# Low parts of FFN weights in a hybrid diffusion step: a subtraction on VectorE replaced by an accumulating DMA

## The chip, the cores and the metric

The kernel runs on one core of a Trainium2 chip. The metric is the device time of one execution in microseconds (us). The profile gives, beside that, the span from the first to the last instruction, and the TensorE clock that was granted in each stretch as a share of full speed.

## What is computed

The reference is one step of a two-layer backbone over 640 tokens (512 latent, 128 context) of width 1024, all in float32. Layer 0 mixes with an S5 scan and neighbourhood attention, layer 1 with a bidirectional SSD scan; after each mixer stands a SwiGLU FFN. The change lies in the FFN alone:

```python
def _swiglu(h, w_gate, w_up, w_down):
    return (jax.nn.silu(h @ w_gate) * (h @ w_up)) @ w_down

# for each layer:
ffn = (ffn_w_gate[layer], ffn_w_up[layer], ffn_w_down[layer])
xs = xs + gtf_s * _swiglu(_modulate(_rmsnorm(xs, norm_ffn_g[layer]), shf_s, scf_s), *ffn)
```

`w_gate` and `w_up` are 1024 x 2816 (22 column blocks of 128), `w_down` is 2816 x 1024.

## The kernel before

TensorE multiplies float32 in a rounded form (F32R). To keep precision, each operand is split in two: a high part `hi` (the value rounded to F32R) and a low part `lo = x - hi`. A product is then three matmuls for each 128-row step k: hi·xh, hi·xl and lo·xh. `split` (L187 to L189) makes the two parts: ScalarE (ACT) copies and rounds to `hi`, then VectorE (DVE) subtracts to get `lo`. Weights arrive from HBM by `raw_w` (L286) into one of two `wraw` buffers, on the queue of SyncE (SP). `split_w` (L291) takes a `whi` and a `wlo` tile, three buffers each, that the whole kernel shares.

Column blocks 0 to 3 of each FFN are computed straightforwardly. Blocks 4 to 21 go through `block_pair` (L438): gate and up of one block are computed together, with the halves of the contraction and of the tokens as the blocks of a 2 x 2 by 2 x 2 product, in seven block products of 12 matmuls (128x128 weights, 320 columns) instead of eight. There are 18 pairs in each layer, 36 in all. A pair loads `rg` (gate) and `ru` (up), 512 KB each; with `a`, `b` the halves of `rg` and `c`, `d` those of `ru` DVE forms the sums `s1 = c+d`, `s2 = s1-a`, `s3 = a-c`, `s4 = b-s2` in single buffers (tiles `fws` and `fsc`). The weights of the seven products are `ab` (`rg` split, 128x1024), `s12` (128x1024), `s34` (two halves, 128x512 each) and `d` (128x512, in its own tile `fwd`). A `whi`/`wlo` pair is free for the next pair's use once both products that read it are done. The token side lies ready in seven forms (`fm`). In the order of the code the products are: ab with forms 0 and 1, s12 with 5 and 4, s34 with 6 and 2, d with 3; ACT and DVE combine their results (`fsc`) and split the gated result into `hb` or `hc`.

Pairs stand in three parts of six for each layer, each followed by the eight down projections over those blocks (`gemm`, L307, which adds into `x` at L398). In layer 0 DVE also computes one adaLN tile (L248) per 512 KB that SP loads into `fws` meanwhile. GpSimd (POOL) sums squares before and after the pairs of a layer, and issues a single small DMA in the whole kernel.

The order of each engine's instructions is fixed at build time by a list scheduler with a timing model of its own; on the chip each engine takes its instructions strictly in that order and waits on semaphores. So a change of a few lines may move instructions on every engine.

Of the kernel before, what the change touches and what calls it, by code (L numbers as in the profile page):

```python
# [8 lines left out]
F32 = mybir.dt.float32  # L9
F32R = mybir.dt.float32r  # L10
BF16 = mybir.dt.bfloat16
AF = mybir.ActivationFunctionType
OP = mybir.AluOpType
# [108 lines left out]
class Kernel:  # L122
# [168 lines left out]
    def split_w(self, raw, nk, mw=128):  # L291
# [2 lines left out]
        self.split(hi[:, :nk, :mw], lo[:, :nk, :mw], raw[:, :nk, :mw])  # L294
        return hi, lo

    def gemm(self, w, xt, nk, n, mw=128, k0=0, total=None, ps=None):
        nc = self.nc
        total = nk if total is None else total
        if ps is None:  # L300
            ps = self.mm.tile([128, 2, 512], F32, name="acc")
        hi, lo = w
        for k in range(nk):
            xh, xl = xt(k0 + k)
            for q, (a, b) in enumerate(((hi, xh), (hi, xl), (lo, xh))):
                for h in range(2):
                    nc.tensor.matmul(ps[:mw, h, :n], a[:, k, :mw], b[:, h * n:(h + 1) * n],  # L307
                                     start=k0 + k == 0 and q == 0, stop=k0 + k == total - 1 and q == 2)
        return ps
# [18 lines left out]
    def xt(self, k):  # L328
        return self.xh[k // 4][:, k % 4], self.xl[k // 4][:, k % 4]
# [108 lines left out]
    def block_pair(self, layer, f, sc, ws, wd, feed):  # L438
        nc = self.nc
        v = nc.vector  # L440
        rg = self.raw_w(self.I["ffn_w_gate"][layer * NFF + f], 8)
        ru = self.raw_w(self.I["ffn_w_up"][layer * NFF + f], 8)
        next(feed, None)
        a, b, c, d = (r[:, i * 4:i * 4 + 4] for r in (rg, ru) for i in range(2))
        s12, s3, s4 = ws
        s1, s2 = s12[:, 0], s12[:, 1]
        ab = self.split_w(rg, 8)
        self.tt(v, s1, c, d, OP.add)
        self.tt(v, s2, s1, a, OP.subtract)
        s12 = self.split_w(s12.rearrange("p i k m -> p (i k) m"), 8)  # L450
        self.tt(v, s3, a, c, OP.subtract)
        self.tt(v, s4, b, s2, OP.subtract)
        hi = self.wpool.tile([128, 8, 128], F32R, name="whi")
        lo = self.wpool.tile([128, 8, 128], F32R, name="wlo")
        self.split(hi[:, :4], lo[:, :4], s3)
        self.split(hi[:, 4:], lo[:, 4:], s4)
        s34 = hi, lo
        self.split(wd[:, 0], wd[:, 1], d)
        acc = self.mm.tile([128, 2, 512], F32, name="acc")
        X, A, Y = acc[:, 0, :TH], acc[:, 1, :TH], self.psum()[:, :TH]  # L460

        def product(ps, w, k0, form, first):
            xh, xl = self.forms[form]
            for k in range(4):
                for q, (m, x) in enumerate(((w[0], xh), (w[0], xl), (w[1], xh))):
                    nc.tensor.matmul(ps, m[:, k0 + k], x[:, k], start=first and k == 0 and q == 0, stop=k == 3 and q == 2, skip_group_check=not first)  # L466

        tu, tg = sc
        t0, t1 = tg[:, :TH], tg[:, TH:]
        next(feed, None)  # L470
        product(X, ab, 0, 0, True)
        nc.scalar.activation(t0, X, AF.Copy)
        product(A, ab, 4, 1, True)
        self.tt(v, t0, A, t0, OP.add)
        product(X, s12, 4, 5, False)
        nc.scalar.activation(t1, X, AF.Copy)
        product(Y, s12, 0, 4, True)
        nc.scalar.activation(tu, Y, AF.Copy)
        product(X, s34, 0, 6, False)
        self.tt(v, tu, X, tu, OP.add)  # L480
        next(feed, None)
        product(Y, s34, 4, 2, False)
        self.tt(v, t1, Y, t1, OP.add)
        nc.scalar.activation(tg, tg, AF.Silu)
        product(X, (wd[:, 0], wd[:, 1]), 0, 3, False)
        self.tt(v, t1, tu, t1, OP.mult)
        self.tt(v, t0, X, t0, OP.mult)
        return tg
# [1068 lines left out]
```

## Time and profile before

| What | Value |
|---|---|
| Time, median of 3 runs | 1913.29 us (1910.25 to 1914.04) |
| The profiled execution's own time | 1918.42 us |
| Its span, first to last instruction | 1916.6 us |
| PE busy | 1820.0 us, 95% |
| DVE busy | 1377.3 us, 72% |
| ACT busy | 888.7 us, 46% |
| POOL busy | 368.8 us, 19% |
| Mean granted TensorE clock | 0.974 |

PE is TensorE's matmul side. Busy shares are means over very different stages; the two FFN stages with pairs run from about 500 to 880 us and from 1540 to 1870 us. An engine that is idle beside a busy PE costs nothing.

### The profile page before, as it was taken

How to read it: one execution, taken by the hardware profiler on the slowest of the kernel's cores; microseconds unless marked ns; L12 is line 12 of the kernel's file. 1: busy time of each engine (PE TensorE's matmuls, PEld its weight loads, DVE VectorE, ACT ScalarE, POOL GpSimd, SP SyncE). 2: the span in 40 equal slices, each digit the busy share in tenths (PEclk: the TensorE clock that was granted, in tenths of full speed). 3: DMA queues.
4: the chain of work that ended last, by engine and by line, in shares of the span. 5: the costliest groups of instructions: out<-in, count | busy, mean ns of one | idle time of the engine just before them, and what ended most of it. 6: DMA issues, size and time to landing. Idle time of an engine off the chain costs nothing.

```text
span 1916.6 us, 31001 instructions
## 1 busy us (share of the span) xinstructions
PE 1820.0 (95%) x12196; PEld 1680.6 (88%) x12196; DVE 1377.3 (72%) x2321; ACT 888.7 (46%) x1541; POOL 368.8 (19%) x425
## 2 busy tenths in 40 slices
PE   4898999899999999999999999998999999999997
PEld 1886777899999999999998788873999999999997
DVE  7879933597796886976777696958546876574754
ACT  5454344536352432444645565655434544252442
POOL 1029800020000000012024444357433000000002
PEclk8998899999999999999999999997999999999999
DMA  7355246532333334343221213135522122222222
GB/s 294 119 139 183 101 143 176 199 110 76 113 126 128 121 130 135 111 143 105 82 78 50 89 50 100 54 130 200 178 79 77 48 97 77 89 79 76 93 70 80
DMA packets 103441, 216.87 MB, mean 113 GB/s; under 512 B 15216, under 2 KB 50688, under 8 KB 102656
## 3 DMA queue, kind: packets, MB, share of 16 engines
q1 hardware_dynamic: 103264, 214.88, 34.5%
q8 instruction: 96, 1.57, 0.3%
q14 instruction: 49, 0.40, 0.1%
q0 software_dynamic: 32, 0.02, 0.0%
HBM read 193.36 MB, written 18.84 MB: 111 GB/s over the span
## 4 chain that ended last, share of the span: by engine, by line
PE 77%; DVE 6%; DMA 3%; issue 2%; ACT 1%; SPq 0%; DVEq 0%; ACTq 0%
PE acc L307 46%; PE acc L466 12%; PE pm L466 5%; DMA fws<-in_ada_w 2%; PE pm L801 2%; DVE junk L248 2%; DVE wlo L189 1%; PE pm L736 1%; PE acc L564 1%; PE pm L564 1%; PE pm L816 1%; DVE fsc L184 1%; PE pm L1211 1%; PE pm L785 1%; PE acc L1392 1%
## 5 line engine op out<-in xcount | busy, mean ns | idle before, releaser
L188 ACT ACTIVATE whi<-wraw 128x1024 fp32r<-128x1024 f32 (+2 forms) x192 | 186.3, 972 | 316.3 <-PE acc L307 214.5
L307 PE MATMUL acc<-xh,whi 128*128 128x322 f32 (+2 forms) x1168 | 287.5, 324 | 8.1 <-ACT xh L1286 6.2
L307 PE MATMUL acc<-xh,wlo 128*128 128x322 f32 (+2 forms) x1168 | 281.6, 319 | 0.0
L307 PE MATMUL acc<-xl,whi 128*128 128x322 f32 (+2 forms) x1168 | 281.2, 319 | 0.0
L184 POOL TENSOR_TENSOR ssq<-ssq 128x640 f32<-128x640 f32 (+2 forms) x45 | 70.0, 1556 | 1093.2 <-ACT ssq L341 654.6
L466 PE MATMUL acc<-fm,whi 128*128 128x320 f32 x1152 | 255.6, 309 | 2.4 <-DVE fsc L184 2.4
L189 DVE TENSOR_TENSOR wlo<-wraw,whi 128x1024 fp32r<-128x1024 f32 (+2 forms) x192 | 218.3, 1138 | 41.1 <-ACT whi L188 40.1
L307 PEld LDWEIGHTS acc<-xh,whi 128*128 128x128 f32 (+1 forms) x1168 | 199.5, 191 | 24.1 <-issue 14.6
L307 PEld LDWEIGHTS acc<-xh,wlo 128*128 128x128 f32 (+1 forms) x1168 | 199.2, 190 | 9.0 <-issue 8.5
L307 PEld LDWEIGHTS acc<-xl,whi 128*128 128x128 f32 (+1 forms) x1168 | 199.7, 191 | 8.0 <-issue 7.6
L466 PEld LDWEIGHTS acc<-fm,whi 128*128 128x128 f32 x1152 | 192.2, 188 | 3.8 <-DVE fsc L184 2.6
L307 PE MATMUL acc<-hb,whi 128*128 128x320 f32 x896 | 171.3, 314 | 8.3 <-DVE x L398 4.0
L466 PE MATMUL acc<-fm,wlo 128*128 128x320 f32 x576 | 177.3, 309 | 0.0
L307 PEld LDWEIGHTS acc<-hb,whi 128*128 128x128 f32 x896 | 142.4, 191 | 11.8 <-DVE fsc L184 4.9
L466 PE MATMUL pm<-fm,whi 128*128 128x320 f32 x576 | 128.3, 308 | 0.0
L398 DVE SCALAR_TENSOR_TENSOR x<-acc,mod,x 128x320 f32<-128x320 f32 (+2 forms) x192 | 72.3, 432 | 65.8 <-PE acc L307 65.6
L669 DVE SCALAR_TENSOR_TENSOR cv<-cv,vecs 128x644 f32<-128x644 f32 x96 | 101.2, 1054 | 19.3 <-ACT cv L667 17.5
L466 PEld LDWEIGHTS acc<-fm,wlo 128*128 128x128 f32 x576 | 108.0, 188 | 0.0
L188 ACT ACTIVATE whi<-fws 128x1024 fp32r<-128x1024 f32 x72 | 60.9, 845 | 100.9 <-PE acc L466 72.3
L307 PE MATMUL acc<-hb,wlo 128*128 128x320 f32 x448 | 103.1, 312 | 0.0
L466 PEld LDWEIGHTS pm<-fm,whi 128*128 128x128 f32 x576 | 96.2, 188 | 0.0
L189 DVE TENSOR_TENSOR wlo<-fws,whi 128x1024 fp32r<-128x1024 f32 x72 | 68.6, 953 | 29.2 <-ACT whi L188 28.7
(384 smaller groups left out, 3803.8 us busy)
## 6 DMA issues: line engine op xcount, KB each, us to landing
wraw<-in_ffn_w_gate SPq DMA_DIRECT2D x44, 512.0 KB, 3.2
wraw<-in_ffn_w_up SPq DMA_DIRECT2D x44, 512.0 KB, 4.0
wraw<-in_od_w_in SPq DMA_DIRECT2D x40, 512.0 KB, 3.3
wraw<-in_ffn_w_down SPq DMA_DIRECT2D x48, 384.0 KB, 3.2
fws<-in_ada_w SPq DMA_DIRECT2D x32, 512.0 KB, 3.3
wlo<-in_ada_n SPq DMA_DIRECT2D x23, 512.0 KB, 4.7
whi<-in_ada_n SPq DMA_DIRECT2D x23, 512.0 KB, 3.7
wraw<-in_ev_w_in SPq DMA_DIRECT2D x16, 512.0 KB, 4.4
```

What stands on the lines that cost most here:

```text
L184: e.tensor_tensor(o, a, b, op=op)
L188: self.nc.scalar.activation(hi, x, AF.Copy)
L189: self.nc.vector.tensor_tensor(lo, x, hi.bitcast(F32), op=OP.subtract)
L248: nc.vector.tensor_tensor_reduce(out=junk, in0=w, in1=self.cond[:, s], scale=1.0, scalar=0.0, op0=OP.mult, op1=OP.add, accum_out=self.mod[ ...
L307: nc.tensor.matmul(ps[:mw, h, :n], a[:, k, :mw], b[:, h * n:(h + 1) * n], start=k0 + k == 0 and q == 0, stop=k0 + k == total - 1 and q == 2)
L398: nc.vector.scalar_tensor_tensor(xk[:, a:b], pv, gate[:, m, s:s + 1], xk[:, a:b], op0=OP.mult, op1=OP.add)
L466: nc.tensor.matmul(ps, m[:, k0 + k], x[:, k], start=first and k == 0 and q == 0, stop=k == 3 and q == 2, skip_group_check=not first)
L564: nc.tensor.matmul(ps[:, :n], w[:, k], x[:, a:b], start=k == 0 and q == 0, stop=k == nf - 1 and q == 2)
L669: nc.vector.scalar_tensor_tensor(acc, cb[:, k:k + G], cw[:, k * 24 + wi:k * 24 + wi + 1], acc, op0=OP.mult, op1=OP.add)
L736: nc.tensor.matmul(ps, Bt[:, c], xw, start=True, stop=True)
L785: nc.tensor.matmul(ps, LH[r], RH[r, hf * 4:hf * 4 + 4].rearrange("p h l -> p (h l)"), start=True, stop=True)
L801: nc.tensor.matmul(ps, at(CT, c), s_in, start=True, stop=True)
```

## The change

In `block_pair` the three weight splits `ab`, `s12` and `s34` go through a new function `split_acc`. ACT first writes the rounded negative, `-hi`, into the low tile, then makes `hi` from it by a second pass with scale -1; then a DMA issued by POOL adds the raw weights onto the low tile in SBUF, which leaves `raw - hi`. The split of `d` and every split outside the pairs stay as they were.

```diff
+    def split_acc(self, *raws):
+        hi = self.wpool.tile([128, 8, 128], F32R, name="whi")
+        lo = self.wpool.tile([128, 8, 128], F32R, name="wlo")
+        k = 0
+        for raw in raws:
+            n = raw.shape[1]
+            h, l = hi[:, k:k + n], lo[:, k:k + n]
+            self.nc.scalar.activation(l, raw, AF.Copy, scale=-1.0)
+            self.nc.scalar.activation(h, l.bitcast(F32), AF.Copy, scale=-1.0)
+            self.nc.gpsimd.dma_start(l, raw, accum_op=OP.add)
+            k += n
+        return hi, lo
...
-        ab = self.split_w(rg, 8)
+        ab = self.split_acc(rg)
         self.tt(v, s1, c, d, OP.add)
         self.tt(v, s2, s1, a, OP.subtract)
-        s12 = self.split_w(s12.rearrange("p i k m -> p (i k) m"), 8)
+        s12 = self.split_acc(s12.rearrange("p i k m -> p (i k) m"))
         self.tt(v, s3, a, c, OP.subtract)
         self.tt(v, s4, b, s2, OP.subtract)
-        hi = self.wpool.tile([128, 8, 128], F32R, name="whi")
-        lo = self.wpool.tile([128, 8, 128], F32R, name="wlo")
-        self.split(hi[:, :4], lo[:, :4], s3)
-        self.split(hi[:, 4:], lo[:, 4:], s4)
-        s34 = hi, lo
+        s34 = self.split_acc(s3, s4)
```

Two places show how the order moves. The first is PE's order in the middle of a part of layer 1, where the next pair's `ab` weights come into use. Before (`acc_17108` is the next pair's accumulator, `whi_17088` and `wlo_17089` its `ab`; `pm_16988` belongs to the pair that is being finished):

```order
L466 MATMUL pm_16988<-fm2_13796,whi_16979 128x320 x2
L466 MATMUL pm_16988<-fm2_13796,wlo_16980 128x320
L466 MATMUL acc_17108<-fm0_13794,whi_17088 128x320 x2
L466 MATMUL acc_17108<-fm0_13794,wlo_17089 128x320
L466 MATMUL acc_17108<-fm0_13794,whi_17088 128x320 x2
L466 MATMUL acc_17108<-fm0_13794,wlo_17089 128x320
```

The low tile is used straight behind the two matmuls with the high one. After the change (`acc_16126` is the next pair's accumulator, `whi_16102` and `wlo_16103` its `ab`; `acc_16001` belongs to the pair that is being finished):

```order
L476 MATMUL acc_16001<-fm5_13871,wlo_15985 128x320
L476 MATMUL acc_16126<-fm0_13866,whi_16102 128x320 x2
L476 MATMUL acc_16001<-fm6_13872,whi_15991 128x320 x2
...
L476 MATMUL acc_16001<-fm6_13872,wlo_15992 128x320
L476 MATMUL acc_16126<-fm0_13866,wlo_16103 128x320
L476 MATMUL acc_16126<-fm0_13866,whi_16102 128x320 x2
```

Between the two matmuls with the new high tile and the first with the new low tile there now stands a whole product of the old pair (form 6, 12 matmuls); in the next pair there are two (forms 2 and 6).

The second place is ACT's order in the same part, over about one pair. Before (`whi<-wraw` is `ab`, `whi<-fws` is `s12` or `s3`, `whi<-fsc` is `s4`; the rest empties PSUM, gates, and splits `d` and the result):

```order
L188 ACTIVATE whi_17209<-wraw_17205 128x1024
L188 ACTIVATE fwd_14531<-wraw_17207 128x512
L188 ACTIVATE hb_13672<-fsc_14529 128x640
L188 ACTIVATE whi_17215<-fws_14530 128x1024
L476 ACTIVATE fsc_14529<-acc_17108 128x320
L472 ACTIVATE fsc_14529<-acc_17229 128x320
L484 ACTIVATE fsc_14529<-fsc_14529 128x640
L188 ACTIVATE whi_17221<-fws_14530 128x512
L188 ACTIVATE whi_17221<-fsc_14529 128x512
```

After the change:

```order
L305 ACTIVATE wlo_16103<-wraw_16098 128x1024
L306 ACTIVATE whi_16102<-wlo_16103 128x1024
L486 ACTIVATE fsc_14601<-acc_16001 128x320
L305 ACTIVATE wlo_16110<-fws_14602 128x1024
L494 ACTIVATE fsc_14601<-fsc_14601 128x640
L306 ACTIVATE whi_16109<-wlo_16110 128x1024
L305 ACTIVATE wlo_16117<-fws_14602 128x512
L305 ACTIVATE wlo_16117<-fsc_14601 128x512
L306 ACTIVATE whi_16116<-wlo_16117 128x512
L482 ACTIVATE fsc_14601<-acc_16126 128x320
L306 ACTIVATE whi_16116<-wlo_16117 128x512
```

Each weight tile is now passed twice, and the passes over the low tile stand first, at the place where the single pass stood. On POOL four DMAs of a pair (`ab`, `s12`, `s3`, `s4`) stand one behind the other, with no other POOL instruction between the first and the last of a layer's 72.

## Rows read from the trace of the kernel before

**Rows 1.** The page, busy time of each engine: us, share of the span, instructions.
```profile
PE 1820.0 (95%) x12196; PEld 1680.6 (88%) x12196; DVE 1377.3 (72%) x2321; ACT 888.7 (46%) x1541; POOL 368.8 (19%) x425
```

**Rows 2.** Windows (us, busy of PE PEld DVE ACT POOL, PEclk, DMA share, GB/s): layer 0, layer 1.
```profile
740.00:800.00 60.00, 60.00 (x410) 59.75 (x409) 50.82 (x87) 25.46 (x39) 0.00 (x0) 1.00 0.35 115
...
1790.00:1850.00 60.00, 60.00 (x412) 60.00 (x411) 44.94 (x71) 31.39 (x48) 0.00 (x0) 1.00 0.26 84
```

**Rows 3.** Chain that ended last, inside the pairs of layer 1: start, us, what.
```profile
1671.01 1.75 PE pm L466 x12
...
1680.09 3.52 PE acc L466 x24
```

**Rows 4.** Groups of PE: busy us, mean ns | idle before, and what ended it.
```profile
L466 PE MATMUL acc<-fm,whi 128*128 128x320 f32 x1152 | 255.6, 309 | 2.4 <-DVE fsc L184 2.4
...
L307 PE MATMUL acc<-hb,whi 128*128 128x320 f32 x896 | 171.3, 314 | 8.3 <-DVE x L398 4.0 <-DVE fsc L184 3.8
...
L466 PE MATMUL acc<-fm,fwd 128*128 128x320 f32 x432 | 72.0, 317 | 5.0 <-DVE fsc L184 5.0
```

**Rows 5.** Waits of ACT, 1560 to 1850 us: total us, times, longest.
```profile
ACT whi L188 <- PE acc L466: 55.5, 42, 3.4
```

**Rows 6.** Groups of DVE by form, pairs of layer 1 (1670 to 1730 us).
```profile
L189 DVE TENSOR_TENSOR wlo<-fws,whi 128x1024 fp32r<-128x1024 f32 x5 | 6.1, 1225 | 8.3 <-ACT whi L188 8.3
L189 DVE TENSOR_TENSOR wlo<-wraw,whi 128x1024 fp32r<-128x1024 f32 x5 | 6.1, 1222 | 1.0 <-ACT whi L188 1.0
...
L189 DVE TENSOR_TENSOR wlo<-fws,whi 128x512 fp32r<-128x512 f32 x5 | 3.5, 690 | 0.1
L189 DVE TENSOR_TENSOR wlo<-fsc,whi 128x512 fp32r<-128x512 f32 x5 | 3.4, 684 | 0.0
```

**Rows 7.** Groups of ACT by form, same stretch.
```profile
L188 ACT ACTIVATE whi<-wraw 128x1024 fp32r<-128x1024 f32 x5 | 5.3, 1061 | 5.5 <-PE acc L466 4.9 <-ACT whi L188 0.6
...
L188 ACT ACTIVATE whi<-fsc 128x512 fp32r<-128x512 f32 x5 | 3.1, 618 | 0.0
```

**Rows 8.** Timeline, the one DMA that POOL issues: start, us.
```profile
175.64 0.71 POOL L1186 DMA_DIRECT2D out_s<-s5x  x1
```

**Rows 9.** Timeline of SP in the pairs of layer 1: two loads of gate weights.
```profile
1699.48 0.33 SPq L288 DMA_DIRECT2D wraw<-in_ffn_w_gate  x1
...
1711.93 0.33 SPq L288 DMA_DIRECT2D wraw<-in_ffn_w_gate  x1
```

**Rows 10.** DMA issues, 1560 to 1850 us: KB each, us from issue to landing.
```profile
wraw<-in_ffn_w_up SPq DMA_DIRECT2D x16, 512.0 KB, 4.4
wraw<-in_ffn_w_gate SPq DMA_DIRECT2D x15, 512.0 KB, 3.3
```

**Rows 11.** Windows (columns as in rows 2): the loads of one pair; copies inside SBUF.
```profile
1790.00:1800.00 10.00, 10.00 (x70) 10.00 (x69) 6.70 (x11) 4.97 (x8) 0.00 (x0) 1.00 0.29 107
...
130.00:140.00 10.00, 6.79 (x76) 6.26 (x75) 9.14 (x7) 4.70 (x14) 8.73 (x7) 0.83 0.99 240
```

**Rows 12.** Waits of the SP queue, 1560 to 1850 us.
```profile
SPq L288 <- DVE wlo L189: 190.2, 29, 10.0
```

**Rows 13.** Windows of layer 0 in which PE had gaps (columns as in rows 2).
```profile
510.00:520.00 10.00, 8.42 (x58) 8.16 (x57) 7.89 (x13) 3.13 (x5) 0.00 (x0) 1.00 0.35 107
...
710.00:720.00 10.00, 7.35 (x29) 6.95 (x30) 7.74 (x13) 1.27 (x2) 0.00 (x0) 0.66 0.32 118
```

## The prediction

> **What bounds the kernel now.** I read the busy times first: PE is busy for 95% of the span, DVE for 72%, ACT for 46%, POOL for 19% [rows 1]. Then the windows over the pairs, the only stage that the diff touches: PE is busy for all 60 us of each, at the full clock, DVE for 75 to 85%, ACT for 42 to 52%, POOL not at all; the 16 DMA engines are busy for 35% of the time in layer 0 and 26% in layer 1 [rows 2]. The chain that ended last runs through PE alone there, 12 matmuls in 1.75 us, so 0.146 us a matmul [rows 3]; a pair is 84 matmuls, 12.25 us, and two gate loads lie 12.45 us apart [rows 9]. So PE sets the pace, and work taken off DVE saves time only where PE waits for DVE. The groups of PE give the whole of that: 2.4 + 3.8 + 5.0 = 11.2 us of idle time ended by DVE on `fsc`, over 36 pairs and their ends [rows 4]. Last, what the weight tiles wait for: ACT stood 42 times before `whi` because PE still read the old tile [rows 5]. Weights are made as soon as a tile is free, and what matters is whether both parts are ready before PE returns to that tile.
>
> **Removed.** Four subtractions a pair on DVE: 1.22 + 1.23 + 0.69 + 0.68 = 3.8 us [rows 6], 138 us over 36 pairs. All of it lies beside a busy PE; its worth is bounded by the 11.2 us above. Those waits stand mostly where a part ends, when DVE has the last pair's combinations and the down projections to do, and a chain of DVE steps would remain; I take half, 5.6 us.
>
> **Added on ACT.** One more pass for each weight tile, two at 1.06 us and two at 0.62 us [rows 7]: 3.4 us a pair. ACT goes from 31.39 us in 60 [rows 2] by 3.4 x 60/12.25 = 16.5 to 48 us, 80%. Queued behind these passes are the copies that empty PSUM and the gating; PE comes back to those accumulators products later, so I cost this at nothing. If PE did stand behind one 0.62 us pass in each pair, that would be 22 us.
>
> **Added on POOL.** Four DMA issues a pair. The one DMA that POOL issued took 0.71 us there [rows 8], SP's issues take 0.33 [rows 9]: 2.8 us in 12.25 on an idle engine, and 0.4 us more of delay in each. Should twice the sources double the issue, 5.7 us still fit, and the delay grows by 0.7. Behind a DMA that waits for ACT stand only the next accumulating DMAs; POOL's sums of squares stand before and behind all pairs of a layer.
>
> **The accumulating DMA itself** is what no row shows. A pair moves 512 KB for `ab`, 512 KB for `s12` and twice 256 KB for `s34`, and for each it has to read the raw part and the low tile and write the low tile. The nearest rows: a plain 512 KB load lands 3.3 us after issue when first in line, 4.4 when another goes ahead [rows 10]. In a stretch with just the two loads of a pair, 107 GB/s for 10 us, the engines were busy for 29% [rows 11]: 2.9 us for two loads, 1.45 us of all 16 engines for 512 KB. Lower bound: the second read is free, 1.45 us. Upper bound: in a stretch with copies from SBUF to SBUF the engines were 99% busy at 240 GB/s [rows 11], 2.16 us for 512 KB; two reads make 4.3 us. I take twice the load's row, 2.9 us, because two operands are read through the same engines, and the loads move the same 512 KB in the same 128 rows of 4 KB. Landing then takes X = 3.3 + 1.45 + 0.4 = 5.15 us alone, and 1.1 us more, 6.25, with a load ahead of it; the bounds give 3.3 + 0.4 = 3.7 and 3.3 - 1.45 + 4.3 + 0.4 = 6.55 alone.
>
> The Trainium skill has a rule that bears on this ("Collectives: The Full Stack", section "Why ReduceScatter is half of AllGather"): an add in the DMA engines needs two read descriptors for each chunk, and ran at 32.35 against 62.28 GB/s for a copy. By that ratio, 1.93, the 1.45 us would become an estimated 2.8 us, and the total below would change by a few us; if the add went at a copy's rate, it would be the first rival. No row here shows either.
>
> **Where it meets the path.** Two loops decide. First, the tile loop for `ab`. In the new PE order I counted, from the release of the low tile (end of form 1) to the first matmul with the new one, 38 and 48 matmuls in alternate pairs of layer 1, and 36 and 46 from there to the next release: on average 43 and 41, 6.3 and 6.0 us. ACT's pass takes 1.06 us of the first, so PE does not wait while X is under 12.25 - 6.0 - 1.06 = 5.2 us. At 5.15 this is even; at 6.25 PE waits 1.05 us in each pair. Second, the engines: a pair needs 3 x 2.9 = 8.7 us for the additions and 2.9 us for its two loads, 11.6 of 12.25 in layer 1. In layer 0, 115 GB/s [rows 2] over 12.25 us are 1.41 MB or 2.7 loads, 3.9 us, so 12.6 us: over the pair by 0.35. With engines 95 to 103% full an addition nearly always meets another transfer, so I take X = 6.2: 1.0 us a pair in layer 1, and 1.0 + 0.35, about 1.3, in layer 0. That is 18 x 1.0 + 18 x 1.3 = 41 us.
>
> New waits and what stands behind them. SP waited 29 times for DVE's low part before it could reload a raw buffer [rows 12]; now it waits for the addition to land, with the load of `up`, and in layer 0 an adaLN tile, queued behind. The loop is 0.33 + 3.3 + 1.06 + 6.2 = 10.9 us, still under 12.25, so no term. DVE waits before `s1` for the addition that reads `s12`, with its additions from PSUM queued behind; counted along PE's order it has some 5 us to spare. The stalls are too short to cost clock: a stretch with PE busy 8.42 of 10 us kept 1.00, one with 7.35 fell to 0.66 [rows 13], and 12.25 us busy in 13.3 is 92%, above the first.
>
> **The sum.** +41 - 5.6 = +35 us. The profiled execution took 1918.4 us with a span of 1916.6, so it would become 1954; it lies 5 us above the median of the runs, 1913.3, which becomes 1948.
>
> **Rivals.** (1) The addition hides, and the kernel is faster. If it goes at a copy's rate, X is 3.7 us and a pair's transfers 3 x 1.45 + 3.9 = 8.3 us: neither loop binds, and DVE's relief closes the waits on `fsc`, 5.6 to 11.2 us: 1902 to 1908. It decides as soon as X stays under 5.2 us and 512 KB cost less than (12.25 - 3.9)/3 = 2.8 us of the engines. For it: the margin missed is small. Against: two operands must be read. (2) The DMA engines become the bound outright. At 4.3 us, a pair takes 12.9 + 2.9 = 15.8 us in layer 1 and 16.8 in layer 0: 18 x 3.6 + 18 x 4.6 = 148 us, 2061. For it: the row of copies inside SBUF. Against: that row mixes in many short transfers. (3) Worse still: additions run at a fraction of a copy's rate, or POOL needs long for the descriptors; each further us for 512 KB adds 3 us a pair, 108 us, and PE's share falls under 78%, near the stretch that lost clock: above 2062. (4) It changes nothing: stalls and relief cancel, 1909 to 1917.
>
> **Chances.** A mild stall, +10 to +75 us, as forecast: 0.40. The addition hidden or nearly so (rivals 1 and 4): 0.30, of which 0.20 is faster by over 0.2% and 0.10 within it; 0.2% is about what a measurement of this kernel can tell from no change. DMA-bound, +75 to +150: 0.18. Beyond: 0.12. So faster 0.20, same 0.10, slower 0.70. The range runs from the full relief of 11 us, 1903, to rival 2, 2062; left out are rival 3 and a few in a hundred below. The forecast's own range is 1923 to 1988.
>
> **What would show it.** Right: PE idle before matmuls of line 476 ended by the DMA on `wlo`, about 1 us a pair, more in layer 0; additions of 512 KB landing in 5 to 7 us; a DMA share of 0.9 or more in the pairs; loads slower than 3.3 and 4.4 us; DVE down by 138 us, ACT up by 122 us. Wrong: no idle time on `wlo` and a DMA share under 0.8 (rival 1), or landings of 8 us and more and PE under 80% (rivals 2 and 3). What would upset it otherwise: ACT's longer queue holding back PSUM, seen as PE waiting for `fsc` on ACT, or the new order moving work outside the FFN.

## The result, and the profile after

The changed kernel took 2038.9 us, the median of 4 runs (2033.0 to 2050.0), against 1913.7 us before (4 runs, 1910.3 to 1918.1): a ratio of 1.066, 95% interval 1.061 to 1.071, or 125 us. The profiled execution took 2033.0 us with a span of 2031.2, at a mean granted clock of 0.968.

The page of the changed kernel, busy time of each engine, answers to [rows 1]; under it the queue of POOL's DMAs with packets, MB and share of 16 engines.

```profile
PE 1850.4 (91%) x12196; PEld 1690.7 (83%) x12196; DVE 1261.5 (62%) x2177; ACT 992.6 (49%) x1685; POOL 492.7 (24%) x569
...
q0 software_dynamic: 20768, 56.65, 15.8%
```

DVE is relieved by 116 us and ACT pays 104 us. PE has the same 12,196 matmuls and is busy 30 us longer, and idle 84 us longer. The queue's share gives the additions' price: 0.158 x 2031.2 = 321 us for 56.65 MB, or 2.97 us of the 16 engines for 512 KB.

What PE waited for in the changed kernel, in all, times, and longest, answers to [rows 4]:

```profile
PE acc L476 <- DVE fsc L184: 28.5, 15, 4.3
PE pm L476 <- DMA wlo<-fws: 19.9, 20, 2.4
...
PE acc L476 <- DMA wlo<-wraw: 13.9, 13, 2.6
PE acc L476 <- ACT fsc L482: 13.1, 6, 4.3
...
PE pm L476 <- DMA wlo<-fsc: 4.0, 6, 1.3
PE acc L476 <- DMA wlo<-fws: 3.5, 3, 1.3
```

New are the waits for the additions: 13.9 us for `ab` and 27.4 us for the sums, 41.3 us in 42 places. New too are the waits for ACT, 22.0 us with three smaller groups (`fsc` and `whi`). The waits for DVE on `fsc`, which the change was to shorten, went from 2.4 + 5.0 us on this line [rows 4] to 28.5: DVE itself now waits 27.7 us for additions before it may write `fws`. These waits name only who came last; a loop that is too long for the pair can show in any of them.

Landings in the changed kernel, median us from issue, answer to [rows 10]:

```profile
wraw<-in_ffn_w_gate SPq DMA_DIRECT2D x44, 512.0 KB, 3.3
wraw<-in_ffn_w_up SPq DMA_DIRECT2D x44, 512.0 KB, 3.7
...
wlo<-wraw POOLq DMA_DIRECT2D x36, 512.0 KB, 5.4
wlo<-fws POOLq DMA_DIRECT2D x36, 512.0 KB, 5.5
```

Windows of the changed kernel (busy of PE, PEld, DVE, ACT, POOL, then PEclk, DMA share, GB/s), two over a part of each layer's pairs as in [rows 2], two short ones:

```profile
510.00:530.00 20.00, 16.50 (x97) 16.43 (x98) 12.17 (x21) 12.47 (x18) 4.22 (x5) 0.83 0.82 186
...
1610.00:1630.00 20.00, 17.23 (x98) 16.97 (x99) 9.70 (x17) 12.18 (x18) 4.33 (x5) 0.83 0.79 171
1740.00:1800.00 60.00, 48.67 (x302) 45.27 (x301) 22.81 (x41) 33.56 (x51) 12.27 (x14) 0.97 0.73 159
740.00:800.00 60.00, 53.37 (x346) 51.95 (x346) 32.86 (x62) 16.68 (x22) 4.38 (x5) 0.96 0.51 147
```

PE was busy for all 60 us of such a window before [rows 2]. The DMA engines are not full: 73% in this window of layer 1. And the clock suffers: with PE busy 16.5 and 17.2 us of 20 it averaged 0.83, that is, about a third of the stretch stood at 1.2 GHz.

Where the time lies can be seen by the matmuls that read a token form, since only the pairs issue them. The view of tile `fm` in layer 1 of the changed kernel (duration min/median/max, first and last start):

```profile
L476 PE MATMUL acc<-fm,whi x576: 302/309/637, 1601.7 to 1974.8; 128*128 128x320 f32 x192
...
L476 PE MATMUL acc<-fm,fwd x216: 302/309/417, 1621.7 to 1979.5; 128*128 128x320 f32 x108
```

From the first to the last start is 377.8 us; the same rows of the kernel before say 1550.5 to 1865.3, 314.8 us. In layer 0 it is 386.9 against 330.6. So the change costs 56 us in layer 0 and 63 in layer 1, 3.1 and 3.5 us a pair, and next to nothing elsewhere. This stretch (down projections between the parts included) is the measure used below.

The chain that ended last shows what a pair now consists of. Changed kernel, layer 1 (start, length, what):

```profile
1768.20 8.00 DMA wlo<-wraw
...
1776.24 1.74 PE acc L476 x10
1777.98 0.29 PE pm L476 x2
1778.27 1.77 PE acc L476 x12
1780.04 1.47 PE pm L476 x10
1781.51 1.77 PE acc L476 x12
...
1783.31 2.43 issue
...
1785.75 4.50 DMA wlo<-wraw
...
1790.29 3.49 PE acc L476 x22
1793.78 0.30 PE pm L476 x2
1794.07 1.77 PE acc L476 x12
...
1795.88 4.71 issue
...
1800.60 4.94 DMA wlo<-wraw
...
1805.56 0.02 SPq L288
...
1805.68 5.78 DMA wraw<-in_ffn_w_up
```

This is a closed loop. PE starts as soon as the addition of `ab` has landed, runs 46 matmuls (7.0 us) to the end of the tile's use, then 2.4 us pass in which ACT remakes the tile ("issue" here is POOL's queue standing behind ACT), and the next addition starts. In the next turn PE runs 36 matmuls (5.6 us), and 4.7 us pass: ACT first splits a result, then remakes the tile by 1798.35, and POOL issues 2.25 us after that. It makes 17.6 and 14.9 us from one issue of `ab` to the next, where a pair of matmuls is 12.25. At 1805 the chain leaves through another door: SP reloads the raw buffer only after the addition has landed. Over the whole stretch of layer 1 (1600 to 1985 us) the chain has several such doors, and none rules:

```profile
by line: PE acc L321 17.8%; PE acc L476 15.5%; DMA wlo<-fws 12.1%; issue 11.7%; DMA wlo<-wraw 10.6%; DMA wraw<-in_ffn_w_up 10.1%; PE pm L476 8.6%; DMA wlo<-fsc 3.7%; PE acc L574 1.6%; DVE fws L184 1.4%; ACT wlo L305 1.4%; DVE fsc L184 1.3%;
```

### The profile page after: what moved, and what is told of

It is laid out like the page before. It is cut to its first block, busy times and chain, and to the rows that moved or that the text cites. A ratio compares the mean times of both kernels' runs of the same rounds, so it can differ in the third digit from the quotient of the medians.

```text
span 2031.2 us, 31490 instructions
## 1 busy us (share of the span) xinstructions
PE 1850.4 (91%) x12196; PEld 1690.7 (83%) x12196; DVE 1261.5 (62%) x2177; ACT 992.6 (49%) x1685; POOL 492.7 (24%) x569
## 3 DMA queue, kind: packets, MB, share of 16 engines
q0 software_dynamic: 20768, 56.65, 15.8%
## 4 chain that ended last, share of the span: by engine, by line
PE 63%; DMA 15%; DVE 5%; issue 5%; ACT 2%; SPq 0%; POOL 0%; DVEq 0%; POOLq 0%; ACTq 0%
PE acc L321 42%; PE acc L476 5%; DMA wraw<-in_ffn_w_up 4%; DMA wlo<-fws 4%; DMA wlo<-wraw 3%; PE pm L476 3%; DMA wlo<-fsc 2%; DMA fws<-in_ada_w 2%; PE pm L811 2%; PE pm L746 1%; DVE junk L248 1%; PE acc L574 1%; PE pm L826 1%; PE pm L574 1%; PE pm L1221 1%
## 5 line engine op out<-in xcount | busy, mean ns | idle before, releaser
L476 PE MATMUL acc<-fm,whi 128*128 128x320 f32 x1152 | 269.5, 322 | 45.6 <-DVE fsc L184 24.5
L188 ACT ACTIVATE whi<-wraw 128x1024 fp32r<-128x1024 f32 (+2 forms) x156 | 147.9, 951 | 260.9 <-PE acc L321 181.9
L476 PEld LDWEIGHTS acc<-fm,whi 128*128 128x128 f32 x1152 | 199.9, 196 | 54.9 <-DVE fsc L184 27.7
L189 DVE TENSOR_TENSOR wlo<-wraw,whi 128x1024 fp32r<-128x1024 f32 (+2 forms) x156 | 173.5, 1115 | 48.5 <-ACT whi L188 48.1
L476 PE MATMUL acc<-fm,wlo 128*128 128x320 f32 x576 | 183.0, 321 | 17.4 <-DMA wlo<-wraw 13.9
L307 POOL DMA_DIRECT2D wlo<-wraw x36 | 31.3, 870 | 526.6 <-ACT whi L306 200.7
L476 PE MATMUL pm<-fm,whi 128*128 128x320 f32 x576 | 134.7, 320 | 1.1 <-ACT fsc L488 1.1
L476 PEld LDWEIGHTS acc<-fm,wlo 128*128 128x128 f32 x576 | 112.1, 195 | 22.6 <-DMA wlo<-wraw 18.0
L307 POOL DMA_DIRECT2D wlo<-fws x72 | 62.6, 869 | 250.0 <-ACT whi L306 144.7
L306 ACT ACTIVATE whi<-wlo 128x1024 fp32r<-128x1024 f32 (+1 forms) x144 | 118.3, 837 | 1.8
L476 PE MATMUL pm<-fm,wlo 128*128 128x320 f32 x288 | 95.4, 331 | 24.1 <-DMA wlo<-fws 19.9
L184 DVE TENSOR_TENSOR fsc<-acc,fsc 128x320 f32<-128x320 f32 x108 | 52.7, 488 | 97.1 <-PE acc L476 96.8
```

Of the source, the lines that this page charges most:

```text
L184: e.tensor_tensor(o, a, b, op=op)
L188: self.nc.scalar.activation(hi, x, AF.Copy)
L189: self.nc.vector.tensor_tensor(lo, x, hi.bitcast(F32), op=OP.subtract)
L306: self.nc.scalar.activation(h, l.bitcast(F32), AF.Copy, scale=-1.0)
L307: self.nc.gpsimd.dma_start(l, raw, accum_op=OP.add)
```

## The experiments

The letters on record stand for these theories. A: ACT's second pass stands ahead of the addition. B: the load on the DMA engines. C: raw and sum buffers are held until the addition lands. D: ACT's longer queue. F: the loop through the raw buffers alone. T: the loop through the weight tile. S: the loop through the sums' single buffers. Three runs of each kernel and a profiled one; "layer 0" and "layer 1" are the stretches defined above, from the profiled execution.

| Kernel | us, median | ratio, 95% interval | layer 0 | layer 1 |
|---|---|---|---|---|
| before | 1913.7 | 1 | 330.6 | 314.8 |
| the change | 2038.9 | 1.061 to 1.071 | 386.9 | 377.8 |
| high part from raw weights | 2048.4 | 1.070 to 1.076 | 393.1 | 382.7 |
| only ab | 1977.5 | 1.033 to 1.036 | 360.3 | 349.2 |
| only the sums | 1985.9 | 1.036 to 1.041 | 375.1 | 338.9 |
| only s12 | 1969.6 | 1.028 to 1.034 | 365.7 | 330.4 |
| plain copy | 1956.8 | 1.022 to 1.027 | 349.0 | 337.9 |
| DVE adds, no DMA | 1922.0 | 1.004 to 1.008 | 334.2 | 313.8 |
| low part first | 2060.4 | 1.076 to 1.081 | 407.5 | 387.3 |
| low part first, plain copy | 1960.5 | 1.024 to 1.028 | 359.2 | 330.0 |
| ab's source HBM | 2062.8 | 1.075 to 1.080 | 401.3 | 382.0 |
| two s12 in layer 1 | 2040.3 | 1.064 to 1.068 | 393.3 | 379.5 |
| both of these | 2055.7 | 1.070 to 1.078 | 397.2 | 386.1 |
| only ab, from HBM | 2029.7 | 1.056 to 1.064 | 385.6 | 377.5 |
| the same, low part first | 2005.2 | 1.046 to 1.049 | 369.7 | 363.5 |
| only ab, from HBM, 4 sets in layer 1 | 1973.8 | 1.027 to 1.033 | 384.3 | 321.4 |
| the change, 4 sets in layer 1 | 2014.7 | 1.052 to 1.055 | 389.8 | 360.1 |
| 4 sets, ab's source HBM | 2019.8 | 1.052 to 1.061 | 398.6 | 350.9 |
| 4 sets, HBM, two s12 | 2020.8 | 1.055 to 1.061 | 398.0 | 356.0 |
| the same, plain copy | 1951.9 | 1.019 to 1.026 | 357.8 | 321.5 |

### Parts alone

**High part from raw weights.** 

> High part made from the raw weights instead of from the low tile, so that the addition no longer has to wait until ACT has read the low tile; all else as in the changed kernel (2039 us). Theory A (the second ACT pass stands between the first pass and the addition in the tile loop, 1.06 us plus a hop in each pair): the additions are issued right behind the first pass, 1.1 to 1.4 us a pair less, so 1990 to 2000 us. Theory B (the DMA engines are full): no change, 2030 to 2045. Theory C (raw and sum buffers are held until the addition lands): the same loop is shorter by 1.1 us too, 1990 to 2005.

```diff
-            self.nc.scalar.activation(h, l.bitcast(F32), AF.Copy, scale=-1.0)
+            self.nc.scalar.activation(h, raw, AF.Copy)
```

2048.4 us, a miss for A, but not a test of it. Freed from its order, the scheduler put the high pass first. ACT's timeline of this kernel:

```profile
1652.16 1.04 ACT L306 ACTIVATE whi<-wraw 128x1024 fp32r<-128x1024 f32 x1
1653.10 1.04 ACT L305 ACTIVATE wlo<-wraw 128x1024 fp32r<-128x1024 f32 x1
```

So the addition still stood behind two passes.

**Only ab** and **only the sums.** Each takes the old split for the other weights.

```diff
-        s12 = self.split_acc(s12.rearrange("p i k m -> p (i k) m"))
+        s12 = self.split_w(s12.rearrange("p i k m -> p (i k) m"), 8)
```

> Only the raw gate weights (ab) go by accumulating DMA, the three sums by the subtraction on DVE: one addition of 512 KB a pair instead of 1.5 MB. Theory B: a third of the DMA load, nothing is left of the loss, 1910 to 1925. Theory A: the ab loop is the tightest and is still there, but the addition lands faster without the others: PE waits 0.5 to 1.5 us a pair, 1930 to 1965. Theory C: the gate buffer is still held until landing: 1940 to 1975.

> Only the sums (s12, s34) go by accumulating DMA, the raw gate weights by the subtraction on DVE: 1 MB of additions a pair. Theory C: the raw buffers come free as before, most of the loss is gone, under 1945. Theory A: the loops of s12 and s34 remain, 0.5 to 2 us a pair, 1935 to 1985. Theory B: two thirds of the load, 9.7 of 12.25 us, nothing is left, 1910 to 1930.

They cost 66 and 74 us, together 140 for 125: near additive. The first lies above all three ranges, the second at A's upper edge and above those of B and C. A third of the bytes costs half of the time, so load on the engines is not the first cause, and the raw buffer, which the sums don't hold, is not the only one.

**Only s12.** The high part from the raw sums, `ab`, `s3` and `s4` split as before. 

> Only s12 by the accumulating transfer (high part from the raw sums); ab, s3 and s4 as before. A third of the bytes of the change. Theory B: a third of the load, engines far from full: 1909 to 1920 us. Theory C (VectorE may write s1 and s2 only when the last addition has read them, and SP's up load queues behind): most of what the two sums cost together, which was 74 us, sits in s12, so 1945 to 1975, with PE waiting for the transfer wlo<-fws. Theory A alone, without the buffers: between, 1920 to 1940.

+58 us, as C had it, with PE waiting 38.2 us for `wlo<-fws`. But T, not yet formed, expects the same: `s12` has a tile of its own that turns once a pair.

**Plain copy.** 

> The accumulating DMA becomes a plain copy of the raw part into the low tile, with the same waits before it; the low part then holds the raw weight, which leaves the subtraction out. If the second read doubles the engine time, the POOL queue's share of the engines falls from 15.8% to about 8% and a 512 KB transfer lands 1.4 us sooner. Theory B: 1915 to 1935. Theory A: one 1.4 us less in each loop, 1980 to 2000. Theory C: as A.

```diff
-            self.nc.gpsimd.dma_start(l, raw, accum_op=OP.add)
+            self.nc.gpsimd.dma_start(l, raw)
```

1956.8 us. Its page shows the queue and the landing:

```profile
q0 software_dynamic: 20768, 56.65, 8.6%
...
wlo<-wraw POOLq DMA_DIRECT2D x36, 512.0 KB, 3.4
wlo<-fws POOLq DMA_DIRECT2D x36, 512.0 KB, 4.2
```

It missed all three, too slow for B and too fast for A and C. PE's and ACT's instructions stand in the very order of the change, so this is the cleanest comparison here: what an addition takes beyond a copy makes 82 of the 125 us. A copy takes 0.086 x 1952.3 us over the same bytes, 1.55 us for 512 KB, and the addition takes 1.91 times as much. The Trainium skill gives 1.93 for a ring collective's copy against its add ("Collectives: The Full Stack", section "Why ReduceScatter is half of AllGather"); this trace agrees with 1.91.

**DVE adds, no DMA.** The two ACT passes stay, DVE adds the raw weights. 

> The two passes of ScalarE stay, but VectorE adds the raw weights onto the low tile, so no transfer inside SBUF is left. Theory A (the second pass stands in the tile loop ahead of a 5.5 us landing): without the landing the chain is 1.06 + 1.06 + 1.22 = 3.3 us, inside the 6 us that PE leaves, so no wait on the weights: 1909 to 1922 us. Theories B and C (DMA engines, buffers held until a landing): the same 1909 to 1922, since their cause is gone. Theory D (ScalarE's longer queue and the new order are what costs, not the transfer): most of the loss stays, 1960 us or more, with PE waiting for ACT on pm, acc or fsc.

```diff
-            self.nc.gpsimd.dma_start(l, raw, accum_op=OP.add)
+            self.nc.vector.tensor_tensor(l, l.bitcast(F32), raw, op=OP.add)
```

1922.0 us, at the upper edge: D's 1960 or more falls. ACT's passes, in the order that this kernel got, cost about 10 us of the 125; the profiled execution (span 1914.3 us) does not show where. That order is not the change's (10,202 of PE's 12,196 matmuls stand at the same place), so what the change's own order costs is not shown apart. The plain copy, which has that order, bounds it: 43 us for the order, ACT's passes and the copy's landing together.

**Low part first.** 

> As the change, but the high part is made from the raw weights and stands behind the negative low part in ScalarE's order, so the addition starts one pass earlier. Theory A: each of 36 pairs gets 1.06 us of the pass and some 0.3 us of hop back, 38 to 49 us: 1990 to 2001 us. Theory B (DMA engines full): the same bytes and no fewer waits, 2030 to 2047. Theory C: the raw and sum buffers also come free a pass earlier, so at least as much as A, and up to one 0.62 us pass more in each pair, 1968 to 2001; the waits of SP and of VectorE for the additions shrink as much as those of PE.

```diff
-            self.nc.scalar.activation(h, l.bitcast(F32), AF.Copy, scale=-1.0)
             self.nc.gpsimd.dma_start(l, raw, accum_op=OP.add)
+            with self.behind(self.nc.scalar):
+                self.nc.scalar.activation(h, raw, AF.Copy)
```

2060.4 us, 22 slower, where A and C both expected a gain and B no change. The addition did start 0.3 us after the low pass. The chain of this kernel now runs, at times, through the raw buffer:

```profile
1635.49 7.09 DMA wlo<-wraw
...
1642.72 5.83 DMA wraw<-in_ffn_w_up
...
1649.17 0.72 ACT hb L188
1649.89 0.95 ACT wlo L305
1650.84 0.96 ACT whi L308
```

The next addition of `ab` is issued at 1651.14, 15.7 us after the first. A loop of the same length stood ready behind the one that was shortened; that became theory F.

**Low part first, plain copy** (the same edit, copying). 

> As the run with the high part behind the low part, but the transfer copies the raw weights onto the low tile and adds nothing (the subtraction is left out), at half the engine time of an addition. Against the plain copy with both passes ahead, 1956.8 us: theory A expects 38 to 45 us back, 1911 to 1920, so that pass and second read together are the whole loss; theory B expects no change from the pass, 1950 to 1960; theory C expects 1911 to 1935.

1960.5 us, where the copy behind both passes took 1956.8: in sum again nothing, so A by itself is not the whole. The table shows what the sum hides: layer 1 gained 8 us and layer 0 lost 10.

### The buffers

**ab's source HBM**, **two s12 in layer 1**, **both**, and **only ab, from HBM.**

```diff
-            self.nc.gpsimd.dma_start(l, raw, accum_op=OP.add)
+            self.nc.gpsimd.dma_start(l, raw if src is None else src, accum_op=OP.add)
...
-        ab = self.split_acc(rg)
+        ab = self.split_acc(rg, src=self.I["ffn_w_gate"][layer * NFF + f].rearrange("p (k m) -> p k m", m=128))
```

```diff
-                    self.split(*ht(f - f0), self.block_pair(layer, f, sc[f % 2], ws, wd[:, f % 2], feed))
+                    two = wb[:, 1536:2560].rearrange("p (i k m) -> p i k m", i=2, k=4) if layer and f % 2 else ws[0]
+                    self.split(*ht(f - f0), self.block_pair(layer, f, sc[f % 2], (two,) + ws[1:], wd[:, f % 2], feed))
```

> As the change, but the addition for ab reads the raw gate weights from HBM a second time and not from the raw buffer, so the raw buffer is free after ScalarE's pass and SP need not wait for the landing. Theory F (the raw loop sets the pace: addition lands, 6.5 us; then gate and, behind it, up is loaded, 5.6 us; then ScalarE's pass over d, the split of the result and the two passes of ab, some 3 us; together about 15 us a pair): this loop is broken, what is left is what the sums cost alone, 1986 us, so 1965 to 1995. Theory T (the tile loop: PE frees the low tile and must wait until the new one is added up, 5.4 us): landing and tile are the same, 2025 to 2047. Theory B (engines full): the same bytes through the engines and more from HBM, 2030 to 2055.

> As the change, but in layer 1 the sums s1 and s2 alternate between two buffers (the second is the space that layer 0 uses for adaLN tiles), so VectorE need not wait for the addition that reads the old sums. Theory S (the sum loop costs): in layer 1 up to half of the 74 us that the sums cost alone, 2000 to 2020 us, and the waits of VectorE before fws for the addition go in layer 1. Theories F, T and B: VectorE has time to spare there, 2030 to 2047.

> Both of the former: the addition for ab reads from HBM, and layer 1 alternates two buffers for s1 and s2. Theories F and S together: layer 1 has neither loop, only layer 0 keeps the sums' loop, 1945 to 1970 us. Theory F alone: as with the HBM source only, 1965 to 1995. Theories T and B: 2025 us or more.

> Only ab by the accumulating transfer, as in the run that took 1977 us, but its source is HBM; s12, s3 and s4 as before the change. Theory F: without the raw loop an addition of 4.9 us fits, 1908 to 1930 us, with PE's waits for wlo on ab (23.8 us there) mostly gone. Theory T: the tile loop is the same, 1965 to 1985. Theory B: far from full in either, so it says nothing here.

They took 2062.8, 2040.3, 2055.7 and 2029.7 us, in the order of the expectations. The gains that F and S promised came in none. T's ranges hold the second and the third, but the first is 16 us and the last 45 us above them, so T's price was wrong too where the source is HBM. The second `s12` was not a clean test: `s3` and `s4` stayed single, and DVE waited for additions before `fws` as long in layer 1 as in the change (19.1 against 18.0 us). The last kernel told the most. Without the raw loop, and with one addition a pair, it lost 63 us in layer 1, as much as the whole change. Its chain there, from 1642 us on, is this and nothing else:

```profile
1642.23 1.07 ACT wlo L305
...
1643.32 1.07 ACT whi L306
1644.39 0.29 issue
1644.67 5.62 DMA wlo<-in_ffn_w_gate
...
1650.34 1.73 PE acc L480 x10
1652.07 1.47 PE pm L480 x10
1653.53 3.53 PE acc L480 x24
...
1657.09 1.07 ACT wlo L305
```

14.9 us from pass to pass: landing 5.6, 44 matmuls 6.7, two passes 2.1, and 0.4 of hops. No other buffer is in it. That is theory T. Other turns of this layer are longer, up to 19.2 us, by later landings (to 8.0 us) and by matmuls at the lower clock: ten that took 1.73 us here took 3.03 or 3.04 us in five turns, and the granted clock from 1753 to 1759 us was 0.50, which is 1.2 GHz.

### The tile loop

**Only ab, from HBM, low part first**: one pass leaves the loop. 

> Only ab by the accumulating transfer with its source in HBM (2029.7 us), but the high part is made from the raw weights and stands behind the negative low part, so one pass of 1.07 us leaves the loop. Theory T (the loop through the weight tile sets the pace: 6.73 us of matmuls from landing to last read, two passes of 1.07, 0.29 to POOL, 5.6 to 5.8 to the landing, some 15 us a pair): 13.9 us a pair, 36 x 1.07 = 38 us less, 1985 to 1997 us. Any theory without that loop: 2020 to 2035.

2005.2 us, 25 of the 38 expected. The loop did lose the pass, but the landing took back a part of it (6.2 and 6.9 us at the place in layer 1 where it was 5.6 to 5.8).

**Only ab, from HBM, 4 sets in layer 1.** A block that lies unused in the pairs of layer 1 becomes a fourth `whi`/`wlo`, taken at every fourth turn.

```diff
+    def wset(self):
+        self.nset += 1
+        if self.nset % 4 or self.spare is None:
+            return [self.wpool.tile([128, 8, 128], F32R, name=n) for n in ("whi", "wlo")]
+        return [self.spare[:, 0], self.spare[:, 1]]
...
+                self.spare, self.nset = self.blk("wsp", [2, 8, 128], F32R) if layer else None, 0
```

> Only ab by the accumulating transfer with its source in HBM (2029.7 us), and in layer 1 a fourth set of weight tiles, in a block that stands unused there, so a tile has a third more time between two uses. Theory T: in layer 1 the loop has 4/3 of a pair, 16.3 us at 12.25 a pair, and 15 fit: PE's waits for wlo on ab go in layer 1 and stay in layer 0; 18 x 2.7 = 49 us less, 1972 to 1990 us. Without that loop: 2020 to 2035.

1973.8 us, within the range of T. Layer 1 goes from 377.5 to 321.4 us, layer 0, which has no fourth set, from 385.6 to 384.3. What PE waited for the addition in layer 1, without and with the fourth set (two kernels):

```profile
PE acc L480 <- DMA wlo<-in_ffn_w_gate: 31.2, 15, 3.3
```

```profile
PE acc L485 <- DMA wsp<-in_ffn_w_gate: 1.4, 1, 1.4
PE acc L485 <- DMA wlo<-in_ffn_w_gate: 1.3, 3, 0.7
```

The addition still takes 5.3 us there and still stands behind two passes; what was changed is the time that the tile may take. The granted clock of the stretch rose with it, from 0.96 to 1.00. With `ab` alone, from HBM, the tile loop is the cause in layer 1.

**The change, 4 sets in layer 1** and **4 sets, ab's source HBM.**

> The whole change with the fourth set of weight tiles in layer 1. If the tile loop T alone sets layer 1's pace: up to half of the 125 us back, 1975 to 1995 us. If the raw loop F (addition of ab 5.4 to 6.9 us, then the loads of gate and up 5.6 to 5.9, then ScalarE's passes) is as long as the tile loop and holds when the tile loop is gone: 2020 to 2045, with SP waiting for the addition's landing as before and PE's waits moved from wlo to fsc and wraw.

> The whole change with the addition for ab from HBM (2062.8 us without more tiles) and the fourth set of weight tiles in layer 1: tile loop and raw loop are both relieved in layer 1, and layer 0 stays as it is. If these two loops are the cause: layer 1 back to 12.3 to 13.5 us a pair, 45 to 70 us less, 1993 to 2018 us. If the engines' load or the sums' single buffer hold as well: 2040 us or more.

2014.7 us, between the two expectations, and 2019.8, just above what both loops together were to leave. In the whole change the fourth set returns 18 of 63 us in layer 1, and with the raw buffer freed early as well 27 of them; 36 us stay. In layer 0, which has no fourth set, freeing the raw buffer cost 9 us.

**4 sets, HBM, two s12** and **the same, plain copy.**

> The whole change with all three loops relieved in layer 1: a fourth set of weight tiles, ab's addition from HBM, and s1 and s2 in two buffers in turn; layer 0 has only the second of them. Theory S (the sums' loop holds the rest): layer 1's stretch of pairs from 351 to 318 to 330 us, the time from 2019.8 to 1987 to 2000 us, no waits of VectorE for the addition on fws in layer 1. Theory B (the engines' load stretches additions and loads to 6 to 7 us, and these then last too long for PE's order): 345 us or more in layer 1, 2010 to 2030 us.

> As the run with all three loops relieved in layer 1, but the transfers copy the raw weights and add nothing (the subtraction is left out), at about half the engine time. Theory B: with 4.3 us less of the engines in each pair landings fall to 3 to 4 us and layer 1 goes back to 315 to 325 us; layer 0 gains too, in all 1920 to 1950 us. Theory S alone: layer 1 as with the additions, within 5 us, and only layer 0 gains.

2020.8 and 1951.9 us. S falls, and B's ranges hold but for 2 us of the second: DVE's waits for additions before `fws` went from 34.0 to 7.4 us in layer 1, the stretch did not shrink (356.0 against 350.9), and the waits for `up` grew. With copies in place of additions layer 1 is at 321.5 us, and layer 0 gains 40. Landings in layer 1 of the two kernels, additions first:

```profile
wraw<-in_ffn_w_up SPq DMA_DIRECT2D x16, 512.0 KB, 6.1
...
wlo<-fws POOLq DMA_DIRECT2D x13, 512.0 KB, 6.3
```

```profile
wraw<-in_ffn_w_up SPq DMA_DIRECT2D x16, 512.0 KB, 4.7
...
wlo<-fws POOLq DMA_DIRECT2D x13, 512.0 KB, 3.7
```

So once the tile loop is open, the rest of layer 1 hangs on what an addition costs beyond a copy: PE waited 25 us for additions in layer 1, and 5 us for copies. Whether by its own longer landing or by the load on the engines that slows `up` too, these runs do not separate. No version with a DMA beat the kernel before.

## Why the prediction was wrong

The direction was right, and so was the kind of cost, PE waiting for additions that land late. The size, +35 for +125 us, was not, and most of what was missing stood in terms put at nothing.

**Right.** The price of the addition (2.9 us of the engines for 512 KB; 2.97 measured), its landing (5.15 alone, 6.25 loaded; 5.4 and 5.5), POOL's issue (0.71 said; 0.87, up to 1.22), and PE idle on `wlo` in front of line 476, somewhat more in layer 0 (22.6 against 18.7 us). DVE fell by 116 where 138 was said and ACT rose by 104 where 122 was. Loads of gate and up were slower only in layer 0 (4.0 and 4.6 us against 3.3 and 4.2); in layer 1 they took 3.3 and 3.7, before 3.3 and 4.3.

**The step that failed: the sum held one tile loop, and that one too short.** It walked the loop through `ab`'s tile alone, 41 us, and gave the tiles of `s12` and `s34`, which turn in the same three buffers, no term. In the runs `ab` alone cost 66 us, the sums alone 74 and `s12` by itself 58. In the changed kernel PE waited 13.9 us for `ab` and 27.4 for the sums; that both together make the 41 us that were said of `ab` is luck.

In `ab`'s loop, PE was not to wait while X is under 12.25 - 6.0 - 1.06 = 5.2 us. The 1.06 is one pass of ACT. But the second pass reads the low tile that the addition will overwrite, so the addition stands behind both. With that pass and 0.3 us to POOL the bound is 3.8 us, and the landings of `ab` were 5.5 us in layer 0 and 5.1 in layer 1, where 6.2 had been taken for X: an estimate of 1.7 and 1.3 us a pair, 54 us. The counts of 36 and 46 matmuls that the 6.0 comes from are those of the chain above. In the kernel with `ab` alone from HBM the order differs, 44 matmuls, and the loop of 14.9 us is 2.6 over the pair; that it binds was shown there by the fourth set. In the whole change the fourth set gave 18 of layer 1's 63 us. For layer 0, which never had one, and for the tiles of the sums alone, the loop is argued and not tested.

**Terms set to nothing.** "Still under 12.25, so no term" for the raw loop counted the gate load and left out `up`, which SP issues behind it, and what stands ahead of ACT's pass: addition 7.1, `up` 5.8, ACT 2.6 make 15.7 us in the run with the low part first. In the changed kernel itself `up` has as much of layer 1's chain as `ab`'s addition (10.1 and 10.6%); freeing the raw buffer on top of four sets gave 9 us in layer 1 (one profile each). ACT's longer queue was costed at nothing too. PE waited 22.0 us for ACT, a sign that the prediction had named as an upset, but 4.6 us in the kernel where DVE adds and ACT has the same passes: ACT stood mostly behind something else, and the trace names `up`, for which it waited 99.4 us before `fwd`, 17.3 before the change. "The stalls are too short to cost clock" failed: PE was busy 30.4 us longer over the same matmuls, a quarter of the loss. It rested on one stretch with 8.42 of 10 us busy at 1.00 [rows 13]; two with 16.5 and 17.2 of 20, shares on either side of it, averaged 0.83.

**The relief that did not come.** Of the 5.6 us by which DVE was to help nothing is seen: the waits on `fsc` grew.

**The engines.** "95 to 103% full" did not come about in layer 1: 11.6 us of transfers in a pair that had become 15.7 us long make 0.74, and the window shows 0.73. Rival 2 gave nearly the right total, 148 us, but by luck: its price of 4.3 us was not there. In layer 0, with adaLN tiles besides, the share was 0.82 at 510 us and 0.51 from 740, and 18 to 29 us stayed there even with copies; what holds it is open.

**Also open:** why the low part first makes the whole change slower by 22 us. ACT's and PE's orders changed with it, and the additions for the sums landed later (6.4 against 5.5 us).

## What to carry to other kernels

Moving work from an engine with slack to a DMA trades throughput for latency. Write down every buffer that the result passes through as a loop: last read, each pass, hop, landing, use until the next last read; take every instruction that touches the buffer, the reader of the half-made value too, and walk every tile that turns, not one. Here three tiles turned once a pair in three buffers, and landings of 5.4 us in place of a 1.2 us subtraction, behind one more pass, cost 3.1 to 3.5 us of a 12.25 us pair. A good test is one more buffer in a place that lies unused. A faster step tells less, since another loop of the same length may stand right behind.

## What the runs showed of the hardware

POOL's issue depends on the kind: 0.87 us for an addition against 0.54 for a copy of the same tile. An addition whose source lies in HBM landed in 6.4 us in layer 1 with `ab` alone (median of 18), against 4.5 with its source in SBUF, at about the same share of the engines (5.5 and 5.2%). Reading from HBM to free a buffer early therefore cost more than the buffer was worth: 2029.7 against 1977.5 us.
